# Input transposes evicted by plain copies, scaled rows made in SBUF, the decay polynomial traced later

## The chip, the core and the metric

The kernel runs on one core of a Trainium2 chip. The metric is the device time of one execution in microseconds (us). Engines are named as in the profile: PE (matrix engine), DVE (vector), ACT (scalar), POOL (GpSimd) and SP, which here only issues DMAs. They run side by side, each through its own instructions in a fixed order, and meet at semaphores.

## What is computed

Two layers of a hybrid trunk over 640 tokens (512 noisy latents and 128 prompt tokens) of width 1024. Cut to what matters here:

```python
def layer(x, cvec, ctx, norm_g, w_mod, b_mod, w_in, ...):
    mod = silu(cvec) @ w_mod + b_mod
    shift, scale, gate = split(mod, 3)
    h = rms_norm(x, norm_g) * (1 + scale) + shift
    rq, rk, rv, rz, q_lat, kv_lat, k_r, ... = split(h @ w_in)
    # three branches: retention, latent attention, Fourier mixing
    ...
    x = x + gate * (merged @ w_out)
```

The retention branch also needs `log_sigmoid(ret_decay_logit)`, 16 numbers.

## The kernel before

All activations are kept transposed: eight tiles of 128 channels by 640 tokens. Every matrix product is made of three passes over a high and a low part of both operands (`hh`, `hl` for the hidden rows, `wh`, `wl` for weights); ACT makes the high part with a cast (L78), DVE or POOL the low part with a subtraction (L74).

The change lies in the opening stage of layer 0. SP loads five token tiles `xn` (L1159, 512 KB each), then, in groups, the first two thirds of `w_mod` in sixteen chunks of 512 KB (`mraw`, L175) and the latents' input weights (`raw`, L92). Then:

- ACT squares each `xn` tile and sums it (L1162); POOL turns the sums into inverse norms `rin` (L1163, L1164).
- PE spreads `rin` over the partitions (`bcast`, L245, five transposes into a PSUM buffer `big`), and ACT copies that to `nR` in SBUF (L247).
- For each of the eight channel blocks d, PE transposes five 128x128 tiles into a `big` buffer (L1170). There are two `big` buffers. ACT copies the block to `xt` (L1172, kept for the residual), and DVE multiplies the same PSUM block by `nR` into `xr` (L1173).
- `mod_use` (L187, L196, L200, L204) multiplies the `w_mod` chunks. Two chunks make one of eight blocks of the shift and scale vectors `modT`: four matmuls for each chunk into the PSUM tile `fill`, a copy by ACT (L192), two small matmuls (L196) and one or two DVE additions.
- `scaled` (L1155) applies scale and shift to `xr`, and `split` makes `hh` and `hl`.
- The latents (`lat_mm`, L85, L86, L87) follow: 120 matmuls of 384 columns for the queries' part, and 120 of 288 columns for the keys' part, with `hh`/`hl` as stationary operand.

Apart from that, the 16 decay logits `lg` go through a chain of some 28 tiny DVE operations and two ACT exponentials (L147 to L169); the results `lgc`, `lg` and `dec` are first read in the retention stage, hundreds of us later.

The order of instructions on each engine is not the order of the code. A scheduler in the build (`schedule_with_timeline_sim=True`) places every instruction by its own estimate of times, by the order in which the code traces them where that leaves a choice. It runs over the whole program, so an edit at the start can also move rows much later. After the build the order is fixed; an engine never passes an instruction that waits.

Of the kernel before, what the change touches and what calls it, by code (L numbers as in the profile page):

```python
# [20 lines left out]
NT = 5
# [9 lines left out]
def build(nc, tc, A, O):  # L31
    ACT, DVE, POOL, PE = nc.scalar, nc.vector, nc.gpsimd, nc.tensor
    root = ExitStack()

    def pool(stack, name, bufs=1, **kw):
        return stack.enter_context(tc.tile_pool(name=name, bufs=bufs, reuse_waits="tile", **kw))

    cp = pool(root, "cp")
# [13 lines left out]
    def big():  # L52
        return psum["p"].tile([P, 1024], F32, name="big", tag="big", bufs=2)
# [67 lines left out]
    prep = pool(pre, "pre")  # L121
# [5 lines left out]
    lg = cp.tile([P, 16], F32, name="lg")  # L127
    nc.scalar.dma_start(lg, A["ret_decay_logit"].rearrange("l d h -> (l d h)").partition_broadcast(P))
    expo = cp.tile([P, 2], F32, name="expo")
# [11 lines left out]
    ACT.activation(cth, cT, AF.Tanh, scale=0.5)  # L141
    DVE.scalar_tensor_tensor(cth, cth, 1.0, cT, op0=ALU.add, op1=ALU.mult)
    DVE.tensor_scalar(cs[:, 0:2 * NK].rearrange("p (k c) -> p k c", c=2), cth.rearrange("p c k -> p k c"), 0.5, None, op0=ALU.mult)


    ab = cp.tile([P, 16], F32, name="ab")
    DVE.scalar_tensor_tensor(ab, lg, -1.0, lg, op0=ALU.mult, op1=ALU.max)  # L147
    ey = cp.tile([P, 16], F32, name="ey")
    ACT.activation(ey, ab, AF.Exp, scale=-1.0)
    DVE.tensor_scalar(ab, ey, 2.0, None, op0=ALU.add)  # L150
    DVE.reciprocal(ab, ab)
    DVE.tensor_tensor(ey, ey, ab, op=ALU.mult)
    DVE.tensor_tensor(ab, ey, ey, op=ALU.mult)
    pl = cp.tile([P, 16], F32, name="pl")
    DVE.memset(pl, 1.0 / 19.0)
    for n in (17, 15, 13, 11, 9, 7, 5, 3, 1):
        DVE.tensor_tensor(pl, pl, ab, op=ALU.mult)
        DVE.tensor_scalar(pl, pl, 1.0 / n, None, op0=ALU.add)
    DVE.scalar_tensor_tensor(pl, pl, -2.0, ey, op0=ALU.mult, op1=ALU.mult)
    DVE.scalar_tensor_tensor(lg, lg, 0.0, pl, op0=ALU.min, op1=ALU.add)  # L160
    lgv = lg.rearrange("p (l d h) -> p l d h", l=2, d=2)
    lgc = cp.tile([P, 2, 2, 2], F32, name="lgc")
    lgp = lg.rearrange("p (l d h e) -> p l d h e", l=2, d=2, e=2)
    for e in range(2):
        DVE.tensor_copy(lgc[64 * e:64 * e + 64], lgp[64 * e:64 * e + 64, :, :, :, e])
    dec = cp.tile([P, 2, 2, 4], F32, name="dec")
    for d in range(2):
        DVE.tensor_scalar(dec[:, :, d, :], lgv[:, :, d, :], expo[:, d:d + 1], None, op0=ALU.mult)
    ACT.activation(dec, dec, AF.Exp)  # L169

    modT = [cp.tile([P, 24, 2], F32, name=f"modT{l}") for l in range(DEPTH)]

# [68 lines left out]
    def bcast(tp, r, t0, t1):  # L241
        a, b = t0 * P, t1 * P
        pb = big()
        for t in range(t0, t1):
            ins = PE.transpose(pb[:, t * P:(t + 1) * P], r[:, t:t + 1].to_broadcast([P, P]), ident)  # L245
        R = tp.tile([P, TT], F32, name="nR", tag="nR", bufs=1)
        ACT.copy(R[:, a:b], pb[:, a:b])  # L247
        return R, ins
# [93 lines left out]
    def lat_w(l, i):  # L342
        return wload(rows(A["w_in"][l], 2 * i, 2, C_LAT, 384), 2, 384, DVE)
# [808 lines left out]
    def scaled(d):  # L1152
        v = xrs[d]
        for c, s_ in ((0, slice(0, T)), (1, slice(T, TT))):
            DVE.tensor_scalar(v[:, s_], v[:, s_], modT[0][:, 8 + d, c:c + 1], modT[0][:, d, c:c + 1], op0=ALU.mult, op1=ALU.add)  # L1155
        split(hh[d], hl[d], v, leng=POOL if d % 2 else DVE)
# [3 lines left out]
    rin = prep.tile([P, NT], F32, name="rin")  # L1160
# [1 line left out]
        ACT.activation(omt.rearrange("p w n -> p (w n)")[:, 0:D], xn[t], AF.Square, scale=D ** -0.5, accum_out=rin[:, t:t + 1])  # L1162
    POOL.tensor_scalar(rin, rin, EPS, None, op0=ALU.add)  # L1163
    POOL.tensor_tensor(rin, rin, mhalf[:, 0:NT], op=ALU.pow)  # L1164
    R, _ = bcast(prep, rin, 0, NT)
    xts, xrs = [], []
    for d in range(NK):
        ps = big()
        for t in range(NT):
            PE.transpose(ps[:, t * P:(t + 1) * P], xn[t][:, d * P:(d + 1) * P], ident)  # L1170
        xt, xr = (prep.tile([P, TT], F32, name=f"{n}{d}") for n in ("xt", "xr"))
        ACT.copy(xt, ps[:, :TT])  # L1172
        DVE.tensor_tensor(xr, ps[:, :TT], R, op=ALU.mult)  # L1173
        xts.append(xt)
        xrs.append(xr)
    for i in range(4):
        for b in (4 + i, i):
            for j in range(0, NK, 4):
                mod_use(0, b, j, mod_load(0, b, j, prep, 256, 256, 4, 10, nc.sync), 256, 4, po1[:, 4 * b:])
        first.append(lat_w(0, i))  # L1180
        for d in (2 * i, 2 * i + 1):
            scaled(d)
    xstore = [nc.sync.dma_start(xd[0][d], xts[d]) for d in range(NK)]
    pre.close()

    acc = None
    for l in range(DEPTH):
# [26 lines left out]
        with ExitStack() as s:  # L1214
# [57 lines left out]
            for n, (idx, src, tmp) in enumerate(((1, omt, None), (0, ort, om), (2, ort, om))):  # L1272
# [5 lines left out]
                for i in range(4):  # L1278
# [14 lines left out]
                    ps = tmp[0:2] if n else ms  # L1293
# [13 lines left out]
        with ExitStack() as s:  # L1307
            xp = pool(s, f"xo{l}")
            xts = []
# [6 lines left out]
            xts = orr + off  # L1316
# [20 lines left out]
            for t0, t1, order in passes:  # L1337
                a, b = t0 * P, t1 * P
                for d in order:
                    xo, xt = om[d % 4], xts[d]  # L1340
                    nc.sync.dma_start(xo[:, a:b], xd[l][d][:, a:b])
                    ps, ins = out_mm(d, a, b)
                    if l + 1 < DEPTH and t0 == 0 and d == order[0]:
                        with tc.issue_after(ins.ins):
                            R, _ = bcast(xp, rms(xp, xts, *passes[0])[0], 2, 5)
                        make_h(l + 1, xp, xts, R, 2, 5)
                    for c, i, j in ((0, a, min(b, T)), (1, T, b)):
                        if j > i:
                            DVE.scalar_tensor_tensor(xt[:, i:j], ps[:, i - a:j - a], modT[l][:, 16 + d, c:c + 1], xo[:, i:j],
                                                     op0=ALU.mult, op1=ALU.add)  # L1350
# [12 lines left out]
                if l + 1 < DEPTH:  # L1363
                    if t0 == 0:
# [13 lines left out]
                        with tc.issue_after(ins.ins):  # L1378
                            R, ins = bcast(xp, r, t0, t1)
# [80 lines left out]
```

## Time and profile before

| what | value |
|---|---|
| median of three runs | 1472.1 us (1469.72 to 1475.49) |
| the profiled execution's own time | 1475.04 us |
| its span, first to last instruction | 1473.3 us |
| PE busy | 1411.6 us (96%) |
| DVE, ACT, POOL busy | 1025.5, 756.2, 239.1 us |
| mean granted PE clock | 0.993 |

PE is the engine to follow: it is busy nearly the whole span. Idle time of another engine costs nothing unless PE waits at its end. In the profile, matmul records overlap, since they are pipelined: the pace is read from one start to the next, not from the duration.

### The profile page before, as it was taken

How to read it: one execution, taken by the hardware profiler on the slowest of the kernel's cores; microseconds unless marked ns; L12 is line 12 of the kernel's file. 1: busy time of each engine (PE TensorE's matmuls, PEld its weight loads, DVE VectorE, ACT ScalarE, POOL GpSimd, SP SyncE). 2: the span in 40 equal slices, each digit the busy share in tenths (PEclk: the TensorE clock that was granted, in tenths of full speed). 3: DMA queues.
4: the chain of work that ended last, by engine and by line, in shares of the span. 5: the costliest groups of instructions: out<-in, count | busy, mean ns of one | idle time of the engine just before them, and what ended most of it. 6: DMA issues, size and time to landing. Idle time of an engine off the chain costs nothing.

```text
span 1473.3 us, 25184 instructions
## 1 busy us (share of the span) xinstructions
PE 1411.6 (96%) x9793; PEld 1345.2 (91%) x9793; DVE 1025.5 (70%) x1896; ACT 756.2 (51%) x1607; POOL 239.1 (16%) x227
## 2 busy tenths in 40 slices
PE   6999999999999999999999999999999999999997
PEld 4989989988988989999999899899889899999997
DVE  5367776666887686698573777765759778779843
ACT  5546666544545453455354566664545445445542
POOL 1220000301102211122312100021110112112240
PEclk9999999999999999999999999999999999999999
DMA  9520003331325474233532100042222433323342
GB/s 317 179 76 1 15 16 98 102 84 33 94 90 176 130 221 129 57 85 92 166 101 84 33 15 16 15 138 77 73 73 65 146 108 104 94 80 86 90 125 87
DMA packets 175847, 138.91 MB, mean 94 GB/s; under 512 B 8304, under 2 KB 168688, under 8 KB 175728
## 3 DMA queue, kind: packets, MB, share of 16 engines
q1 hardware_dynamic: 157680, 120.16, 28.1%
q10 hardware_dynamic: 18048, 17.15, 3.7%
q8 instruction: 77, 1.26, 0.4%
q14 instruction: 42, 0.34, 0.1%
HBM read 125.98 MB, written 11.30 MB: 93 GB/s over the span
## 4 chain that ended last, share of the span: by engine, by line
PE 74%; DVE 12%; DMA 5%; ACT 4%; issue 4%; POOL 1%; SPq 0%; POOLq 0%; ACTq 0%; DVEq 0%
PE bank L1109 25%; PE sm L85 6%; PE sm L87 5%; PE sm L86 5%; PE big L269 4%; PE bank L1080 4%; PE big L513 4%; PE fill L319 3%; PE sm L319 3%; PE sm L534 2%; PE sm L526 2%; DVE wl L74 2%; PE fill L187 2%; DMA raw<-in_w_in 1%; PE big L411 1%
## 5 line engine op out<-in xcount | busy, mean ns | idle before, releaser
L74 DVE TENSOR_TENSOR wl<-raw,wh 128x1024 fp32r<-128x1024 f32 (+5 forms) x146 | 153.8, 1055 | 87.3 <-ACT wh L78 39.0
L78 ACT CAST wh<-raw 128x1024 fp32r<-128x1024 f32 (+5 forms) x126 | 104.7, 833 | 86.2 <-DMA raw<-in_w_in 27.9
L1109 PE MATMUL bank<-hh,wh 128*128 128x320 f32 x416 | 130.0, 315 | 5.5 <-ACT tg L1125 4.4
L85 PE MATMUL sm<-wh,hh 128*128 128x256 f32 (+2 forms) x456 | 134.2, 295 | 0.5 <-DVE vl L74 0.5
L86 PE MATMUL sm<-wl,hh 128*128 128x256 f32 (+2 forms) x456 | 133.8, 294 | 0.0
L87 PE MATMUL sm<-wh,hl 128*128 128x256 f32 (+2 forms) x456 | 132.6, 294 | 0.0
L1109 PE MATMUL bank<-hl,wh 128*128 128x320 f32 x416 | 128.6, 310 | 0.0
L1109 PE MATMUL bank<-hh,wl 128*128 128x320 f32 x416 | 127.1, 311 | 0.0
L74 POOL TENSOR_TENSOR wl<-raw,wh 128x1024 fp32r<-128x1024 f32 (+1 forms) x32 | 66.4, 2075 | 294.9 <-ACT wh L78 215.7
L74 POOL TENSOR_TENSOR wl<-st,wh 128x512 fp32r<-128x512 f32 x26 | 38.0, 1463 | 328.8 <-ACT wh L78 328.8
L85 PEld LDWEIGHTS sm<-wh,hh 128*128 128x128 f32 x456 | 87.8, 193 | 2.2 <-issue 0.8
L1109 PEld LDWEIGHTS bank<-hh,wh 128*128 128x128 f32 x416 | 78.3, 188 | 11.9 <-ACT tg L1125 5.2
L86 PEld LDWEIGHTS sm<-wl,hh 128*128 128x128 f32 x456 | 87.8, 193 | 0.1
L87 PEld LDWEIGHTS sm<-wh,hl 128*128 128x128 f32 x456 | 87.4, 192 | 0.4 <-issue 0.4
L1109 PEld LDWEIGHTS bank<-hl,wh 128*128 128x128 f32 x416 | 78.5, 189 | 0.0
L1109 PEld LDWEIGHTS bank<-hh,wl 128*128 128x128 f32 x416 | 78.0, 189 | 0.0
L74 DVE TENSOR_TENSOR ptl<-sm,pth 128x384 fp32r<-128x384 f32 x128 | 67.2, 549 | 13.9 <-ACT pth L78 12.9
L1109 PE MATMUL bank<-bq,wh 128*128 128x320 f32 x320 | 72.0, 311 | 0.0
L78 ACT CAST pth<-sm 128x384 fp32r<-128x384 f32 x128 | 57.2, 481 | 22.6 <-PE sm L526 21.8
L78 ACT CAST wh<-st 128x512 fp32r<-128x512 f32 x68 | 39.6, 618 | 55.1 <-PE bank L1109 53.7
L640 DVE TENSOR_REDUCE nm<-big 128x1 f32<-128x768 f32 x64 | 60.7, 948 | 1.7 <-PE big L513 1.6
L74 DVE TENSOR_TENSOR wl<-st,wh 128x512 fp32r<-128x512 f32 x42 | 40.8, 972 | 29.5 <-ACT wh L78 27.0
(578 smaller groups left out, 4540.3 us busy)
## 6 DMA issues: line engine op xcount, KB each, us to landing
raw<-in_w_in SPq DMA_DIRECT2D x96, 512.0 KB, 4.0
mraw<-in_w_mod ACTq DMA_DIRECT2D x32, 512.0 KB, 4.0
raw<-in_w_branch SPq DMA_DIRECT2D x24, 512.0 KB, 3.6
mraw<-in_w_mod SPq DMA_DIRECT2D x16, 512.0 KB, 9.2
raw<-in_w_out SPq DMA_DIRECT2D x16, 512.0 KB, 4.3
raw<-in_w_in SPq DMA_DIRECT2D x8, 384.0 KB, 6.1
om<-xd SPq DMA_DIRECT2D x16, 192.0 KB, 3.5
xd<-xt SPq DMA_DIRECT2D x8, 320.0 KB, 4.2
```

Source lines behind the costliest of these rows:

```text
L74: eng.tensor_tensor(lo, src, hi.bitcast(F32), op=ALU.subtract)
L78: ACT.copy(hi, src)
L85: PE.matmul(out, ah, bh, start=first, stop=False)
L86: PE.matmul(out, ah, bl, start=False, stop=False)
L87: return PE.matmul(out, al, bh, start=False, stop=last)
L187: PE.matmul(ps[c:c + 32, :n], cs[:, 2 * (j + i):2 * (j + i) + 32], rv[:, i, :], start=(j + i < 4), stop=(j + i >= 4), tile_position=(0, c))
L269: PE.matmul(ps[:, 512 * h:512 * h + 320], ws[a][:, k, :], xs[b][k][:, 320 * h:320 * h + 320], start=(first and k == 0 and i == 0), stop=(l ...
L319: PE.matmul(ps, w[a][:, k, :], (hh, hl)[b][k][:, hs], start=(k == 0 and i == 0), stop=(k == NK - 1 and i == 2))
L513: PE.matmul(S[:, 512 * h:512 * h + 384], qT[hd][a][:, t * P:(t + 1) * P], (kth, ktl)[b][hd % 3][:, 384 * h:384 * h + 384], start=(i == 0), ...
L640: DVE.tensor_reduce(nm, Sv, axis=AX.XY if len(Sv.shape) == 3 else AX.X, op=ALU.max, negate=True)
L1080: PE.matmul(A, ws[u][:, k, j * P:(j + 1) * P], xs[k][v][:, h, :], start=(k == 0 and i == 0), stop=(k == 3 and i == 2))
L1109: PE.matmul(ps, w[u], x[v], start=(first and k == 0 and j == 0), stop=(k == n - 1 and j == 2), skip_group_check=True)
```

## The change

Three edits, all traced in the opening stage:

1. The block loop no longer multiplies out of PSUM. Each transposed block is only copied to `xt`, by ACT for odd d and by DVE for even d.
2. `bcast` is traced after the eight blocks, and eight DVE multiplications then make `xr` out of `xt` in SBUF.
3. The decay logits' chain is traced after the loop over the `mod_use` blocks and the latents' weights, no longer before everything.

```diff
-    ab = cp.tile([P, 16], F32, name="ab")
-    DVE.scalar_tensor_tensor(ab, lg, -1.0, lg, op0=ALU.mult, op1=ALU.max)
...
-    ACT.activation(dec, dec, AF.Exp)
...
-    R, _ = bcast(prep, rin, 0, NT)
     xts, xrs = [], []
     for d in range(NK):
         ps = big()
         for t in range(NT):
             PE.transpose(ps[:, t * P:(t + 1) * P], xn[t][:, d * P:(d + 1) * P], ident)
         xt, xr = (prep.tile([P, TT], F32, name=f"{n}{d}") for n in ("xt", "xr"))
-        ACT.copy(xt, ps[:, :TT])
-        DVE.tensor_tensor(xr, ps[:, :TT], R, op=ALU.mult)
+        if d % 2:
+            ACT.copy(xt, ps[:, :TT])
+        else:
+            DVE.tensor_copy(xt, ps[:, :TT])
         xts.append(xt)
         xrs.append(xr)
+    R, _ = bcast(prep, rin, 0, NT)
+    for d in range(NK):
+        DVE.tensor_tensor(xrs[d], xts[d], R, op=ALU.mult)
     for i in range(4):
...
+    ab = cp.tile([P, 16], F32, name="ab")
+    DVE.scalar_tensor_tensor(ab, lg, -1.0, lg, op0=ALU.mult, op1=ALU.max)
...
+    ACT.activation(dec, dec, AF.Exp)
```

What the scheduler makes of it shows at three places. In the rows, `xn_87` to `xn_91` are the five token tiles, `fill<-mraw` is one chunk of `w_mod` (x4: its four matmuls), `sm<-sel,mraw` the small matmuls that close a block. Line numbers of the changed kernel differ: L1143 is L1170 of before, L161 is L187, L170 is L196, L219 is L245, L1153 is L1173, L1129 is L1155.

PE, the first matmuls of the program, before:

```order
L133 MATMUL sm<-ident,vecs 128x128
L187 MATMUL fill<-mraw,cs 32x256 x4
L245 MATMUL big<-ident,rin 128x128 x5
L1170 MATMUL big<-ident,xn_87 128x128
L1170 MATMUL big<-ident,xn_88 128x128
```

and after:

```order
L133 MATMUL sm<-ident,vecs 128x128
L1143 MATMUL big<-ident,xn_87 128x128 x2
L1143 MATMUL big<-ident,xn_88 128x128 x2
L1143 MATMUL big<-ident,xn_89 128x128 x2
L1143 MATMUL big<-ident,xn_90 128x128 x2
L1143 MATMUL big<-ident,xn_91 128x128 x2
```

The transposes of the first two blocks now stand ahead of the first chunk of `w_mod` and of `bcast`.

PE, where the latents' matmuls begin (`hh_149` and `hh_112` are the same tile, `hh0`), before:

```order
L196 MATMUL sm<-sel,mraw 128x2 x2
L187 MATMUL fill<-mraw,cs 32x256 x4
L85 MATMUL sm<-wh,hh_149 128x384
L86 MATMUL sm<-wl,hh_149 128x384
L85 MATMUL sm<-wh,hh_149 128x384
L86 MATMUL sm<-wl,hh_149 128x384
L1170 MATMUL big<-ident,xn_87 128x128
```

and after:

```order
L170 MATMUL sm<-sel,mraw 128x2 x2
L161 MATMUL fill<-mraw,cs 32x256 x8
L219 MATMUL big<-ident,rin 128x128 x5
L170 MATMUL sm<-sel,mraw 128x2 x2
L161 MATMUL fill<-mraw,cs 32x256 x8
L170 MATMUL sm<-sel,mraw 128x2 x2
L161 MATMUL fill<-mraw,cs 32x256 x16
L85 MATMUL sm<-wh,hh_112 128x384
```

Before, the first latent matmul stood behind the seventh chunk of `w_mod` and with three blocks of transposes still to come; after, it stands behind the twelfth chunk and behind all transposes.

DVE, the rows up to the first scaling of a hidden row, before:

```order
L1173 TENSOR_TENSOR xr_211<-big,nR 128x640
L200 TENSOR_TENSOR modT_147<-sm,vT 128x4
L204 SCALAR_TENSOR_TENSOR modT_147<-modT_147,vT 128x4
L74 TENSOR_TENSOR wl<-raw,wh 128x768
L1173 TENSOR_TENSOR xr_221<-big,nR 128x640
L200 TENSOR_TENSOR modT_147<-sm,vT 128x4
L1155 TENSOR_SCALAR xr_211<-xr_211,modT_147 128x512
```

and after:

```order
L1153 TENSOR_TENSOR xr_166<-xt_165,nR 128x640
L1153 TENSOR_TENSOR xr_175<-xt_174,nR 128x640
L1153 TENSOR_TENSOR xr_184<-xt_183,nR 128x640
L1153 TENSOR_TENSOR xr_193<-xt_192,nR 128x640
L1153 TENSOR_TENSOR xr_202<-xt_201,nR 128x640
L1153 TENSOR_TENSOR xr_211<-xt_210,nR 128x640
L1153 TENSOR_TENSOR xr_220<-xt_219,nR 128x640
L1153 TENSOR_TENSOR xr_229<-xt_228,nR 128x640
L1129 TENSOR_SCALAR xr_166<-xr_166,modT_110 128x512
```

The scaling of the first block stood behind two multiplications by `nR`; it now stands behind all eight.

The decay chain's 28 DVE rows have kept their place near the start of DVE's order, with one copy of a transposed block (`xt_165`) among the last of them; the exponential of `dec` on ACT stands one copy later than before. SP's order up to the latents' weights is the same in both. From the latents to the end of layer 0's attention PE's rows are the same in both; from the Fourier stage on, and in layer 1, rows of the branch products and of the later `mod_use` chunks differ in places by some rows to some dozen.

## Rows read from the trace of the kernel before

**Rows 1.** The page: the span of the profiled execution.

```profile
span 1473.3 us, 25184 instructions
```

**Rows 2.** Windows: stretch, length, busy us (instructions) of each engine, clock, DMA share, GB/s.

```profile
0.00:14.30 14.30, 0.45 (x1) 0.18 (x1) 5.95 (x35) 7.35 (x13) 0.93 (x8) 1.00 0.77 263
14.30:34.20 19.90, 19.45 (x165) 13.87 (x166) 13.77 (x26) 11.73 (x21) 3.19 (x4) 1.00 1.10 351
34.20:72.35 38.15, 38.15 (x282) 35.85 (x281) 14.13 (x28) 18.26 (x42) 12.20 (x23) 1.00 0.59 197
72.35:100.00 27.65, 27.05 (x170) 25.96 (x168) 17.46 (x39) 13.65 (x25) 5.92 (x6) 1.00 0.28 81
```

**Rows 3.** Timeline of PE: start us, us, engine, line, operation, tiles, count, idle before.

```profile
14.41 1.08 PE L187 MATMUL fill<-mraw,cs 128*32 128x256 f32 x8 [11.13 <-DVE dec L168]
16.84 1.27 PE L1170 MATMUL big<-ident,xn 128*128 128x128 f32 x5
18.64 0.77 PE L1170 MATMUL big<-ident,xn 128*128 128x128 f32 x5
25.67 0.44 PE L85 MATMUL sm<-wh,hh 128*128 128x384 f32 x1
39.09 0.33 PE L87 MATMUL big<-wh,hl 128*128 128x384 f32 x1
41.00 0.34 PE L86 MATMUL big<-wl,hh 128*128 128x384 f32 x1
72.35 1.25 PE L403 MATMUL sm<-ident,latq 128*128 128x128 f32 x9
```

**Rows 4.** Timeline of SP's queue: issue start, us, of three chunks of `w_mod`.

```profile
16.68 1.42 SPq L175 DMA_DIRECT2D mraw<-in_w_mod  x1
22.50 1.34 SPq L175 DMA_DIRECT2D mraw<-in_w_mod  x1
23.96 1.35 SPq L175 DMA_DIRECT2D mraw<-in_w_mod  x1
```

**Rows 5.** DMA issues of those chunks, the first alone, then two: KB, us to landing.

```profile
mraw<-in_w_mod SPq DMA_DIRECT2D x1, 512.0 KB, 9.2
mraw<-in_w_mod SPq DMA_DIRECT2D x2, 512.0 KB, 9.7
```

**Rows 6.** Lines on DVE and ACT, 14 to 60 us: busy us, mean ns, idle.

```profile
L1173 DVE TENSOR_TENSOR xr<-big,nR 128x640 f32<-128x640 f32 x8 | 6.5, 816 | 4.6 <-ACT xt L1172 4.6
L1155 DVE TENSOR_SCALAR xr<-xr,modT 128x512 f32<-128x512 f32 x8 | 4.3, 542 | 0.1
L1155 DVE TENSOR_SCALAR xr<-xr,modT 128x128 f32<-128x128 f32 x8 | 2.7, 340 | 0.0
L74 DVE TENSOR_TENSOR hl<-xr,hh 128x640 fp32r<-128x640 f32 x4 | 3.3, 817 | 0.1
L78 ACT CAST hh<-xr 128x640 fp32r<-128x640 f32 x8 | 5.6, 732 | 2.4 <-DVE xr L1155 2.4
L247 ACT COPY nR<-big 128x640 f32<-128x640 f32 x1 | 0.7, 693 | 2.6 <-PE big L245 2.6
```

**Rows 7.** Lines on PE, 15.6 to 75 us: busy us, mean ns, idle.

```profile
L187 PE MATMUL fill<-mraw,cs 128*32 128x256 f32 x120 | 9.0, 390 | 0.0
L1170 PE MATMUL big<-ident,xn 128*128 128x128 f32 x40 | 6.5, 298 | 0.0
L196 PE MATMUL sm<-sel,mraw 128*128 128x2 f32 x32 | 4.3, 237 | 0.1
```

**Rows 8.** Windows of PE: a sparse stretch of the attention, and what follows.

```profile
100.00:103.00 3.00, 1.36 (x6) 1.00 0.66 177
103.00:107.00 4.00, 3.83 (x11) 0.57 0.04 8
```

**Rows 9.** Windows of the stages whose order also differs, columns as in rows 2.

```profile
300.00:450.00 150.00, 142.11 (x978) 133.27 (x977) 114.13 (x246) 71.73 (x158) 15.67 (x20) 0.99 0.28 78
450.00:475.00 25.00, 21.62 (x159) 19.03 (x159) 18.14 (x31) 12.26 (x24) 6.06 (x4) 1.00 0.58 179
```

More of the change, by code (lines that the diff above doesn't have):

```diff
@@ L143, in build @@
     DVE.tensor_scalar(cs[:, 0:2 * NK].rearrange("p (k c) -> p k c", c=2), cth.rearrange("p c k -> p k c"), 0.5, None, op0=ALU.mult)
-    ab = cp.tile([P, 16], F32, name="ab")
-    DVE.scalar_tensor_tensor(ab, lg, -1.0, lg, op0=ALU.mult, op1=ALU.max)
[L148 to L168, printed above, removed]
-    ACT.activation(dec, dec, AF.Exp)
     modT = [cp.tile([P, 24, 2], F32, name=f"modT{l}") for l in range(DEPTH)]
@@ L1182, in build @@
             scaled(d)
+    ab = cp.tile([P, 16], F32, name="ab")
+    DVE.scalar_tensor_tensor(ab, lg, -1.0, lg, op0=ALU.mult, op1=ALU.max)
+    ey = cp.tile([P, 16], F32, name="ey")
+    ACT.activation(ey, ab, AF.Exp, scale=-1.0)
+    DVE.tensor_scalar(ab, ey, 2.0, None, op0=ALU.add)
+    DVE.reciprocal(ab, ab)
+    DVE.tensor_tensor(ey, ey, ab, op=ALU.mult)
+    DVE.tensor_tensor(ab, ey, ey, op=ALU.mult)
+    pl = cp.tile([P, 16], F32, name="pl")
+    DVE.memset(pl, 1.0 / 19.0)
+    for n in (17, 15, 13, 11, 9, 7, 5, 3, 1):
+        DVE.tensor_tensor(pl, pl, ab, op=ALU.mult)
+        DVE.tensor_scalar(pl, pl, 1.0 / n, None, op0=ALU.add)
+    DVE.scalar_tensor_tensor(pl, pl, -2.0, ey, op0=ALU.mult, op1=ALU.mult)
+    DVE.scalar_tensor_tensor(lg, lg, 0.0, pl, op0=ALU.min, op1=ALU.add)
+    lgv = lg.rearrange("p (l d h) -> p l d h", l=2, d=2)
+    lgc = cp.tile([P, 2, 2, 2], F32, name="lgc")
+    lgp = lg.rearrange("p (l d h e) -> p l d h e", l=2, d=2, e=2)
+    for e in range(2):
+        DVE.tensor_copy(lgc[64 * e:64 * e + 64], lgp[64 * e:64 * e + 64, :, :, :, e])
+    dec = cp.tile([P, 2, 2, 4], F32, name="dec")
+    for d in range(2):
+        DVE.tensor_scalar(dec[:, :, d, :], lgv[:, :, d, :], expo[:, d:d + 1], None, op0=ALU.mult)
+    ACT.activation(dec, dec, AF.Exp)
     xstore = [nc.sync.dma_start(xd[0][d], xts[d]) for d in range(NK)]
```

## The prediction

> **What bounds the kernel now.** I read the page first, then a table of windows over the opening stage, then PE's timeline in it, and last the DMA queue. The span is 1473.3 us [rows 1], the profiled execution took 1475.0 us, which is 2.9 us over the median of 1472.1, so what I add to the one I add to the other. The windows show two different limits in the first 72 us [rows 2]. Up to 14.3 us PE has done 0.45 us of work; it waits for its first chunk of `w_mod`. From 14.3 to 34.2 us the sixteen DMA engines are full (share 1.10, 351 GB/s), and PE is busy too, 19.45 of 19.9 us. From 34.2 to 72.35 us PE is busy without a gap, 38.15 of 38.15 us, and the DMA share has fallen to 0.59. The last latent matmul ends where the first transpose of `latq` starts, at 72.35 us [rows 3], and PE then goes on nearly without idle time, 27.05 of 27.65 us up to 100 us [rows 2]. So the time at which PE ends the latents is handed on to everything behind, nearly one to one. The whole change is judged by that one time.
>
> Two things in PE's timeline matter for it [rows 3]. The first latent matmul starts at 25.67 us: before, the latents are mixed with the transposes and with the chunks of `w_mod` that have already landed, so PE always has work while chunks are on their way. And the first work is slow: five transposes take 1.27 us at 16.84 us and 0.77 us at 18.64 us.
>
> **The change part by part.** *Transposes earlier.* The forty transposes now need only the token tiles and a free PSUM buffer. Ten of them start as the tiles land, up to 12.9 us, in time in which PE was idle. The other thirty start from some 14 us on. That takes work forward out of the stage from 14.3 us on. It is worth something only if PE then has something else to do earlier, and that is the question.
>
> *Where the first latent matmul stands.* In PE's new order it stands behind the twelfth chunk of `w_mod`, before it stood behind the seventh. PE cannot pass a waiting row, so no latent matmul starts before the twelfth chunk has landed. SP's order there is unchanged and the DMA engines are full, so I take the landings from the trace. The eighth chunk is issued at 16.68 us and lands 9.2 us later, at 25.9 us; the eleventh and twelfth are issued at 22.50 and 23.96 us and land 9.7 us later, at 32.2 and 33.7 us [rows 4, 5]. One chunk costs PE 9.0 us / 15 = 0.60 us [rows 7]. So the first latent matmul cannot start before 33.7 + 0.6 = 34.3 us, against 25.67.
>
> *What PE has to do meanwhile.* All transposes, `bcast`, eight chunks and four of the small closing steps stand ahead. From 14.2 us these are six blocks of transposes at some 0.7 us (4.2), eight chunks (4.8), `bcast` (0.7) and four closings of about 0.5 (4.3 us / 8 [rows 7]), 11.7 us in all and perhaps 2 more while PE is slow: PE is through with them about when the eighth chunk has been used and closed, at 27.2 us. From there to 34.3 us it has four chunks of 0.6 us, 2.4 us of work in 7 us.
>
> *The sum at 34.3 us.* What counts is the work that is left then. Before, 24 of the 240 latent matmuls were done by 34.2 us (4, 6, 2 and 12 rows of PE's order); after, none. They are of the 384-column kind, whose pace is (41.00 - 39.09) / 11 = 0.174 us [rows 3], so 24 are 4.2 us. Against that, before still had six chunks ahead and the new order has four: 2 x 0.60 = 1.2 us less. The closings left are four in both. Net: 4.2 - 1.2 = **+3.0 us** at PE's full rate.
>
> *PE's clock.* [...] I take **+1.7 us**, with nothing as the low end and twice that as the high end. [...]
>
> *`xr` from SBUF.* A 128x640 multiplication out of PSUM takes 816 ns, a subtraction of the same size wholly in SBUF 817 ns [rows 6], so the eight cost the same, 6.5 us. They now stand in one row behind `nR`. Their pace is about 0.74 us, since records overlap, so `hh0` is ready 8 x 0.74 (5.9), one scaling pair (0.54 + 0.34 = 0.88, some 0.75 by pace) and the cast (0.73) after `nR`, 7.4 us. `nR` comes when `bcast` and a 0.69 us copy are done. `bcast` stands behind six chunks, two closings and all transposes: 14.2 + 4.2 + 3.6 + 1.0 + 2 us for the slow start = 25.0 us, then 0.7 for itself and 0.7 for the copy: 26.4 us, so `hh0` at 33.8 us. This is half a us before 34.3 us: hidden by the wait for the twelfth chunk, but only just.
>
> *Four copies from ACT to DVE.* About 0.8 us each (as the 816 ns above); ACT and DVE both have room before 26 us (11.7 and 13.8 of 19.9 us [rows 2]). Nothing.
>
> *The decay chain.* Its DVE rows keep their place, in time in which DVE waits for `xn`, and its results are read in the retention stage. Nothing.
>
> *Later rows.* From the Fourier stage on the order differs by some rows. PE is idle 7.9 us between 300 and 450 us and 3.4 us between 450 and 475 us [rows 9]; a shift of rows can win or lose a part of this, and I take 0 with 2 us either way. What could swallow the delay is idle time of PE before that, 0.6 us up to 100 us [rows 2].
>
> Sum: 3.0 + 1.7 = 4.7 us, so 1475.0 + 4.7 = 1479.7 us for a profiled execution like the one shown, and 1472.1 + 4.7 = **1476.8 us** for the median. That is 0.32%. About 0.5%, 7.4 us, is what a measurement of this kernel can tell from no change, so the likeliest result is no change that can be told, on the slow side.
>
> **The rivals.** *DVE's row of eight becomes the bound (slower).* If `nR` comes later than 26.9 us, `hh0` and not the twelfth chunk starts the latents, and every further us is a us of the total. The mechanism is PE's slow start: at 1.27 in place of 0.77 us for a block and 1.08 us for a chunk [rows 3], thirty transposes and six chunks would take 7.6 + 6.5 us, not 4.2 + 3.6, if the clock stayed down up to `bcast`. Then `nR` comes at 14.2 + 14.1 + 1.0 + 1.4 = 30.7 us, `hh0` at 38.1 us, 3.8 us after the chunk. Price: 3.0 + 1.7 + 3.8 = 8.5 us, 1480.6 us. For it: only half a us of cover, and two PSUM buffers whose release now alternates between ACT and DVE, where a late one stalls the next block. Against it: before, PE was at full rate at 18.04 us or so after 3.6 us of work, and its work here is as dense.
>
> *The early transposes win (faster).* If chunks landed sooner than PE gets to them, the transposes' work, 6.5 us of records [rows 7], some 5.6 us by pace, would leave the full stretch: 1466.5 us. Against it: the landings, which hang on 351 GB/s of a full DMA system [rows 2], and nothing in the change moves a byte.
>
> *The clock holds.* Then only +3.0 us: 1475.1 us.
>
> *The change does nothing.* The delay is swallowed by idle time between 100 and 475 us, where PE waits on other engines: 1472 us. Those waits hang on work that is itself delayed, so I give it little.
>
> **How the numbers follow.** Forecast as summed, 0.45, with the later rows' 2 us either way: about a sixth of it ends beyond 7.4 us. Clock holds 0.17. DVE bound, in full or in part, 0.20, nearly all beyond 7.4 us. Nothing 0.12. Early transposes win 0.06, of which most is beyond 0.5%. Slower: 0.07 + 0.18 = 0.25. Faster: 0.05. Same: 0.70. The range has to leave out 2 in 10: from 1470.5 us (nothing, with the later rows winning) to 1483 us (DVE bound in full, with the later rows losing); outside lie the early transposes' win, a part of the case of nothing, and the worst of DVE's case.
>
> **What would show it.** In the changed kernel's profile: transposes at 7 to 13 us; PE busy about a third from 27 to 34 us, with rows of `w_mod` matmuls each waiting for a DMA; the first latent matmul (L85) at 34.3 us, with the twelfth chunk as the last thing waited for; a granted clock near one half for some 3 to 4 us around there; the first transpose of `latq` at 77 us in place of 72.35. If L85 starts at 34 us but waits for ACT's `hh`, DVE was the bound. If it starts well before 33 us, my landings or the reading of the order are wrong, and the prediction with them. If `latq` comes at 77 us and the total is unchanged, the delay was swallowed later.

## The result and the profile after

The changed kernel takes 1481.31 us in the median (1479.08 to 1485.22), the kernel before beside it 1471.56 us. The ratio is 1.0070, with a 95% interval of 1.0054 to 1.0086; by the medians it is 9.8 us or 0.66% slower. The time lies in the range that was given. It is twice the step that was forecast, though, and the forecast's likeliest case, no change that can be told, did not come.

The profiled execution of the changed kernel took 1484.34 us. The page gives its span (before: [rows 1]):

```profile
span 1482.5 us, 25171 instructions
```

The windows of the opening, columns as in [rows 2] (stretch, length, then busy us and count of PE, PEld, DVE, ACT and POOL, granted clock, DMA share, GB/s):

```profile
0.00:14.30 14.30, 3.99 (x12) 1.74 (x13) 5.68 (x31) 7.66 (x14) 0.95 (x8) 1.00 0.78 261
14.30:27.00 12.70, 11.56 (x111) 7.32 (x111) 6.93 (x18) 5.31 (x12) 1.23 (x2) 1.00 1.10 353
27.00:34.20 7.20, 5.09 (x37) 1.61 (x38) 7.20 (x14) 2.63 (x5) 0.96 (x1) 0.54 1.09 349
34.20:38.00 3.80, 3.80 (x16) 3.25 (x20) 3.80 (x8) 2.42 (x4) 1.62 (x2) 0.50 1.10 351
38.00:42.00 4.00, 4.00 (x22) 3.30 (x14) 0.48 (x1) 0.83 (x1) 1.88 (x1) 0.60 0.81 269
42.00:77.00 35.00, 35.00 (x245) 33.97 (x245) 11.17 (x24) 15.70 (x38) 11.13 (x22) 1.00 0.45 147
```

Before 14.3 us PE now does 4 us of work instead of 0.45. From 27 to 34.2 us it is busy 5.1 of 7.2 us, and at a clock of 0.54, so this is not even 3 us of work at the full rate. From 34.2 us on PE is busy without a gap, but up to 42 us at 0.50 and 0.60, against 1.00 behind that. (The clock column reads 1.00 in the first rows too, but PE still runs at half pace there: a chunk takes 1.08 us at 15.46 us and 0.64 us at 17.54 us. I do not use the column before 18 us.)

PE's timeline of the changed kernel (start us, us, engine, line, operation, tiles, count, idle before; L161 is the `w_mod` chunk, L170 the small matmuls that close a block, L85 and L86 the latents, L219 `bcast`, L377 the first transpose of `latq`; before: [rows 3]). Each matmul of a chunk and of a closing counts twice in the profile, so a chunk's four show as x8:

```profile
23.48 0.76 PE L219 MATMUL big<-ident,rin 128*128 128x128 f32 x5
...
25.91 0.64 PE L161 MATMUL fill<-mraw,cs 128*32 128x256 f32 x8 [0.69 <-DMA mraw<-in_w_mod]
27.04 0.61 PE L170 MATMUL sm<-sel,mraw 128*128 128x2 f32 x4 [0.49 <-ACT mraw L166]
28.54 1.08 PE L161 MATMUL fill<-mraw,cs 128*32 128x256 f32 x8 [0.90 <-DMA mraw<-in_w_mod]
29.96 1.08 PE L161 MATMUL fill<-mraw,cs 128*32 128x256 f32 x8 [0.34 <-DMA mraw<-in_w_mod]
31.57 1.08 PE L161 MATMUL fill<-mraw,cs 128*32 128x256 f32 x8 [0.53 <-ACT mraw L166]
32.96 1.08 PE L161 MATMUL fill<-mraw,cs 128*32 128x256 f32 x8 [0.31 <-DMA mraw<-in_w_mod]
33.97 0.69 PE L85 MATMUL sm<-wh,hh 128*128 128x384 f32 x1
...
36.27 0.52 PE L85 MATMUL big<-wh,hh 128*128 128x384 f32 x1
36.59 0.52 PE L86 MATMUL big<-wl,hh 128*128 128x384 f32 x1
...
41.32 0.34 PE L86 MATMUL sm<-wl,hh 128*128 128x384 f32 x1
41.49 0.34 PE L87 MATMUL sm<-wh,hl 128*128 128x384 f32 x1
...
78.48 1.25 PE L377 MATMUL sm<-ident,latq 128*128 128x128 f32 x9
```

The chunks come one by one, and PE waits before each; at 31.57 us it is ACT's copy of the block before (L166) that ends the wait, at the others the DMA. The first latent matmul starts at 33.97 us, right behind the twelfth chunk. Neighbouring latent matmuls stand 0.32 us apart at 36 us and 0.17 us apart at 41 us: the same instruction at a granted clock of 0.50 (36 to 37 us) and of 1.00 (41.2 to 42 us). `latq` follows at 78.48 us, against 72.35 before: **+6.1 us**. By this reading 6.1 of the 9.8 us are lost in the opening, and the other 3.6 us come later.

DVE's timeline of the changed kernel in that stretch, and ACT's casts that make the first two `hh` (columns as above; L1153 is `xr` from SBUF, L1129 the scaling):

```profile
25.00 5.97 DVE L1153 TENSOR_TENSOR xr<-xt,nR 128x640 f32<-128x640 f32 x8
30.89 1.51 DVE L1129 TENSOR_SCALAR xr<-xr,modT 128x512 f32<-128x512 f32 x4
33.99 2.74 DVE L1129 TENSOR_SCALAR xr<-xr,modT 128x512 f32<-128x512 f32 x4
...
31.73 1.44 ACT L78 CAST hh<-xr 128x640 fp32r<-128x640 f32 x2 [0.24 <-DVE xr L1129]
```

The eight multiplications run in one row, and the first scaling follows at 30.89 us. ACT's two casts are done at 33.17 us, the first of them, `hh0`, about 0.7 us earlier. What PE's first latent matmul reads at 33.97 us has by then been ready for more than 1 us, so DVE is not what the latents wait for.

### The profile page after: what moved, and what is told of

Same layout as the page of the kernel before. It is cut to its first block, busy times and chain, and to the rows that moved or that the text cites. A ratio compares the mean times of both kernels' runs of the same rounds, so it can differ in the third digit from the quotient of the medians.

```text
span 1482.5 us, 25171 instructions
## 1 busy us (share of the span) xinstructions
PE 1420.9 (96%) x9793; PEld 1349.2 (91%) x9793; DVE 1028.9 (69%) x1900; ACT 755.7 (51%) x1603; POOL 240.2 (16%) x227
## 4 chain that ended last, share of the span: by engine, by line
PE 75%; DVE 11%; DMA 5%; ACT 4%; issue 4%; POOL 1%; SPq 0%; POOLq 0%; ACTq 0%; DVEq 0%
PE bank L1083 26%; PE sm L85 6%; PE sm L87 6%; PE sm L86 6%; PE bank L1054 4%; PE big L487 4%; PE fill L293 3%; PE big L243 3%; PE sm L293 3%; PE sm L508 3%; PE sm L500 2%; PE fill L161 2%; DVE wl L74 2%; DMA s<-in_state_ret 1%; PE big L385 1%
## 5 line engine op out<-in xcount | busy, mean ns | idle before, releaser
L85 PE MATMUL sm<-wh,hh 128*128 128x256 f32 (+2 forms) x456 | 135.6, 298 | 1.0 <-DVE vl L74 0.9
L86 PE MATMUL sm<-wl,hh 128*128 128x256 f32 (+2 forms) x456 | 135.3, 297 | 0.0
L85 PEld LDWEIGHTS sm<-wh,hh 128*128 128x128 f32 x456 | 88.8, 195 | 2.9 <-DVE vl L74 1.4
L86 PEld LDWEIGHTS sm<-wl,hh 128*128 128x128 f32 x456 | 88.9, 195 | 0.1
```

Source lines behind the costliest of these rows:

```text
L85: PE.matmul(out, ah, bh, start=first, stop=False)
L86: PE.matmul(out, ah, bl, start=False, stop=False)
```

## The experiments

**Theory.** The changed kernel loses by the place of the first latent matmul in PE's fixed order (behind the twelfth chunk of `w_mod`, which lands at 33 us) and by the clock that the thin stretch before it brings down. **Rival:** the edits cost by themselves: copies on DVE, multiplications out of SBUF, the polynomial. A second question came with the totals: what are the 3.6 us behind `latq`?

The median of each kernel (5 to 12 runs) stands beside that of runs of the kernel before on the same chip; e9_before_rows and e10_lazy ran on a second chip. The ratio is not taken from the medians, so the two can differ by 1 us or so. "Rest" is the difference of the medians less the shift of `latq`. `latq` is read in one profiled execution of each kernel, and three kernels with the same order on every engine (changed, e2_nopoly, e10_lazy) have it 1.2 us apart, so a rest is good to some 2 us and no better.

| kernel | first latent behind chunk | first latent, us | `latq`, us (shift) | median less before | ratio (95%) | rest |
|---|---|---|---|---|---|---|
| before | 7 | 25.67 | 72.35 | | | |
| changed | 12 | 33.97 | 78.48 (+6.1) | +9.8 | 1.0070 (1.0054 to 1.0086) | +3.6 |
| e1_poly | 7 | 25.65 | 72.33 (0.0) | -0.3 | 1.0005 (0.9992 to 1.0018) | -0.3 |
| e2_nopoly | 12 | 34.79 | 78.67 (+6.3) | +9.4 | 1.0073 (1.0054 to 1.0091) | +3.1 |
| e3_gate | 12 | 33.72 | 74.15 (+1.8) | +6.2 | 1.0051 (1.0033 to 1.0068) | +4.4 |
| e4_warm | 12 | 34.93 | 77.09 (+4.7) | +2.6 | 1.0024 (1.0012 to 1.0035) | -2.1 |
| e5_copies | 8 | 28.29 | 73.08 (+0.7) | +1.7 | 1.0007 (0.9997 to 1.0017) | +1.0 |
| e6_held | 9 | 29.98 | 75.64 (+3.3) | +5.2 | 1.0039 (1.0024 to 1.0055) | +1.9 |
| e7_held_b1 | 7 | 25.96 | 72.89 (+0.5) | +1.5 | 1.0009 (0.9996 to 1.0021) | +0.9 |
| e8_held_b3 | 8 | 26.52 | 73.42 (+1.1) | +2.1 | 1.0020 (1.0008 to 1.0032) | +1.0 |
| e9_before_rows | 7 | 25.62 | 75.78 (+3.4) | +7.5 | 1.0049 (1.0037 to 1.0061) | +4.1 |
| e10_lazy | 12 | 34.12 | 77.50 (+5.2) | +8.5 | 1.0053 (1.0040 to 1.0066) | +3.4 |
| e11_bcast | 8 | 26.34 | 71.02 (-1.3) | -0.6 | 1.0003 (0.9989 to 1.0018) | +0.7 |

### One edit at a time: the polynomial

e1_poly is the kernel before with this alone:

```diff
-    ab = cp.tile([P, 16], F32, name="ab")
...
-    ACT.activation(dec, dec, AF.Exp)
...
         for d in (2 * i, 2 * i + 1):
             scaled(d)
+    ab = cp.tile([P, 16], F32, name="ab")
...
+    ACT.activation(dec, dec, AF.Exp)
```

> The kernel before with the third edit alone: the decay polynomial is traced behind the latents' inputs, nothing else is changed. PE's first latent matmul stands behind the seventh chunk of w_mod, as before. Theory (the place of the first latent matmul and the clock after the sparse stretch make the loss): the first transpose of latq at 72.4 us as before, ratio 1.000, within 2 us of the kernel before, by later rows alone. Rival (the polynomial's move costs, through the rows that it moves later): some +2 to +4 us of the 9.75, ratio 1.002 or more, and that from after 900 us.

e2_nopoly is the changed kernel with the polynomial back at its old place.

> The changed kernel with the polynomial back in its old place: edits 1 and 2 alone. PE's first latent matmul stands behind the twelfth chunk. Theory: opening as in the changed kernel, first latent matmul at 34.0 us and latq at 78.5 us, ratio 1.007 (1.004 to 1.009). Rival (the polynomial is a part of it): ratio about 1.004 with latq at 78.5 us, or latq well before 78.5 us.

Measured: 1.0005 and 1.0073, `latq` at 72.33 and 78.67 us. PE's order is in e1_poly that of before and in e2_nopoly that of the changed kernel. The polynomial is worth nothing that these runs can tell, and the loss belongs to edits 1 and 2.

### The place alone

e3_gate is the kernel before, with nothing but an order: the latents' matmuls of `hh0` are put behind the twelfth chunk.

```diff
+        if l == 0 and b == 2 and j == 4:
+            twelfth[1] = twelfth[0]
...
-                    lat_mm(acc[t], t, k, *w[k // 2], k % 2)
+                    if k == 0:
+                        with tc.issue_after(twelfth[1].ins):
+                            lat_mm(acc[t], t, k, *w[k // 2], k % 2)
```

> The kernel before with no edit to copies, multiplications or polynomial; only the first latent matmuls (those of hh0) are held behind the last matmul of the twelfth chunk in PE's order. Theory: the place alone makes the loss. First latent matmul at 34.0 to 34.3 us; the work left is then as in the changed kernel, +3.0 us, so latq at 75.4 us if the clock holds (here transposes are spread up to the tenth chunk, so PE is less idle before 34 us) and at up to 78.5 us if it falls as in the changed kernel; ratio 1.002 to 1.006. Rival (the row of eight multiplications on DVE, or the copies, delay the latents): without them nothing is lost, latq within 1 us of 72.4, ratio 1.000.

PE's timeline and windows of e3_gate (L1177 transposes, L188 a chunk, L199 a closing, L85 the first latent matmul, L410 the first transpose of `latq`):

```profile
28.78 0.77 PE L1177 MATMUL big<-ident,xn 128*128 128x128 f32 x5 [0.85 <-DVE xr L1180]
31.38 0.61 PE L199 MATMUL sm<-sel,mraw 128*128 128x2 f32 x4 [0.49 <-ACT mraw L195]
33.15 0.64 PE L188 MATMUL fill<-mraw,cs 128*32 128x256 f32 x8 [0.59 <-DMA mraw<-in_w_mod]
33.72 0.44 PE L85 MATMUL sm<-wh,hh 128*128 128x384 f32 x1
74.15 1.26 PE L410 MATMUL sm<-ident,latq 128*128 128x128 f32 x9
```

```profile
27.00:34.20 7.20, 5.07 (x53) 3.29 (x54) 6.52 (x14) 4.54 (x9) 1.78 (x2) 1.00 1.09 351
34.20:38.00 3.80, 3.80 (x28) 3.79 (x30) 0.96 (x1) 0.91 (x2) 0.78 (x1) 1.00 1.10 351
```

The first latent matmul again comes at 33.72 us, behind the same chunk, although nothing was changed on copies or multiplications. The clock is 1.00 throughout. PE has more to do in the thin stretch here (53 rows from 27 to 34.2 us where the changed kernel has 37), since some transposes stand later in this order. The place without the clock costs 1.8 us, less than the 3.0 that I had put down and far less than the changed kernel's 6.1. So the place is one part, and the clock, which stayed up here, can be the other. The whole is nevertheless 6.2 us slower: the rest, +4.4 us, is the largest of all, with an order of the later rows that is neither that of before nor that of the changed kernel.

### Work added to keep the clock up

e4_warm is the changed kernel with 16 matmuls more, of chunks 8 to 11 into an unused half of a PSUM buffer:

```diff
+    spare = []
...
+        if l == 0 and (b, j) in ((1, 4), (6, 0), (6, 4), (2, 0)):
+            for i in range(kk):
+                c = 32 * i
+                PE.matmul(spare[1][c:c + 32, 512:768], cs[:, 2 * (j + i):2 * (j + i) + 32], rv[:, i, :], start=True, stop=True,
+                          tile_position=(0, c))
...
+    spare += [big(), big()]
```

> The changed kernel with added work: the matmuls of chunks 8 to 11 of w_mod are done a second time into an unused half of a PSUM buffer, 16 matmuls more, 2.4 us at full rate, in the time in which PE waits for the next chunk; the first latent matmul stays behind the twelfth chunk. Theory (the sparse stretch from 27 to 34 us lets the clock fall, and its return at 41 us costs 3.1 us): granted clock near 1.00 from 27 to 41 us, first latent matmul at 34.0 to 34.6 us, latq at 75.4 us, so the whole 3 us faster than the changed kernel, ratio to the kernel before about 1.0045, although there is more work. Rival (the half pace from 34 to 41 us has another cause than PE's idle time): the clock stays near 0.5 there, latq at 78.5 us or later by up to 1.2 us, ratio 1.007 or more.

PE's timeline and windows of e4_warm (L162 a chunk, L167 the added matmuls):

```profile
30.16 0.61 PE L167 MATMUL big<-mraw,cs 128*32 128x256 f32 x8
32.42 0.64 PE L167 MATMUL big<-mraw,cs 128*32 128x256 f32 x8 [1.65 <-DMA mraw<-in_w_mod]
33.92 1.08 PE L162 MATMUL fill<-mraw,cs 128*32 128x256 f32 x8 [0.42 <-DMA mraw<-in_w_mod]
34.93 0.69 PE L85 MATMUL sm<-wh,hh 128*128 128x384 f32 x1
```

```profile
27.00:34.20 7.20, 4.06 (x60) 1.98 (x60) 7.20 (x13) 2.59 (x5) 0.02 (x1) 0.97 1.09 351
34.20:38.00 3.80, 3.80 (x24) 3.06 (x20) 3.50 (x8) 1.93 (x4) 2.23 (x1) 0.61 1.10 351
38.00:42.00 4.00, 4.00 (x30) 3.59 (x27) 3.22 (x4) 0.54 (x1) 1.84 (x1) 1.00 0.85 261
```

The clock stays at 0.97 up to 34.2 us and is back by 38 us. In between it falls, after PE has waited 1.65 us for the eleventh chunk. The added matmuls read the chunk that they repeat, so they stand beside that chunk's own and none was left for this wait. So `latq` came at 77.09 us, not at the 75.4 us expected. Still, with more work it came 1.4 us sooner than in the changed kernel, although its latents began 1.0 us later (34.93 us). The low stretch was shorter: 3.8 x 0.39 = 1.5 us lost, against 3.8 x 0.50 + 4.0 x 0.40 = 3.5 us, an estimate from the windows. That the whole is 7.1 us faster than the changed kernel (+2.6 against +9.8) has another part, which lies behind `latq` (rest -2.1 against +3.6); its later rows, too, have an order of their own.

### Do the copies and the multiplications cost?

e5_copies is the kernel before with edit 1 alone; the multiplication stays in the loop, and `bcast` ahead of it:

```diff
-        ACT.copy(xt, ps[:, :TT])
-        DVE.tensor_tensor(xr, ps[:, :TT], R, op=ALU.mult)
+        if d % 2:
+            ACT.copy(xt, ps[:, :TT])
+        else:
+            DVE.tensor_copy(xt, ps[:, :TT])
+        DVE.tensor_tensor(xr, xt, R, op=ALU.mult)
```

> The kernel before with the copies alone: the blocks are copied to xt by ACT and DVE in turn, and xr is made from xt in SBUF, but each multiplication stays in the block loop and bcast stays ahead of it. In PE's order the transposes are all done after the tenth chunk of w_mod, and the first latent matmul stands behind that. Theory (the place of the first latent matmul decides): the tenth chunk lands near 30.7 us, so the latents begin some 5 us later than before, but with all transposes done; latq at 72.5 to 75 us. Rival (SBUF multiplications and copies on DVE cost by themselves): latq at 76 us or later, with PE waiting for xr or hh before the latents and not for a DMA.

The text has the place wrong: the first latent matmul stands behind the eighth chunk there, not the tenth. It started at 28.29 us, `latq` came at 73.08 us (+0.7), and the ratio is 1.0007. The rival asked for 76 us or later. Copies and multiplications out of SBUF cost next to nothing here.

e11_bcast is the changed kernel with a single line moved; all three edits stay:

```diff
-    R, _ = bcast(prep, rin, 0, NT)
...
+        if d == 1:
+            R, _ = bcast(prep, rin, 0, NT)
```

> The changed kernel with one line moved: bcast is traced behind the second block of transposes, not behind the eighth; copies, the row of eight multiplications out of SBUF traced behind the loop, and the polynomial's new place all stay. PE's first latent matmul then stands behind the eighth chunk of w_mod with all transposes ahead of it, and PE's order from the latents' end on is that of the kernel before, row for row. Theory (the changed kernel loses by the place of the first latent matmul, the clock behind it and the later rows' order, not by the copies and multiplications): first latent matmul near 26.5 us, clock 1.00, latq at 71 to 73.5 us, ratio 0.999 to 1.002. Rival (the copies and SBUF multiplications, or the polynomial's place, are what costs): latq at 76 us or later, ratio over 1.004.

PE's timeline, the windows and DVE's group for `xr` in e11_bcast (the group: partitions x elements, count | busy us, mean ns of one | idle before):

```profile
25.77 0.64 PE L161 MATMUL fill<-mraw,cs 128*32 128x256 f32 x8 [0.20 <-DMA mraw<-in_w_mod]
26.34 0.44 PE L85 MATMUL sm<-wh,hh 128*128 128x384 f32 x1
71.02 1.25 PE L377 MATMUL sm<-ident,latq 128*128 128x128 f32 x9
```

```profile
14.30:27.00 12.70, 12.31 (x115) 8.23 (x116) 10.21 (x25) 6.33 (x13) 1.18 (x1) 1.00 1.10 352
27.00:34.20 7.20, 7.11 (x51) 5.98 (x50) 6.97 (x12) 2.69 (x5) 3.79 (x2) 1.00 1.10 350
```

```profile
L1154 DVE TENSOR_TENSOR xr<-xt,nR 128x640 f32<-128x640 f32 x8 | 6.4, 820 | 2.4 <-ACT nR L221 2.4
```

This decides between the two. With `bcast` behind the second block of transposes, `nR` is there early, the latents begin at 26.34 us, PE is busy 7.11 of 7.2 us at a clock of 1.00 where the changed kernel was busy 5.09 at 0.54, and `latq` comes 1.3 us sooner than in the kernel before. The whole is 1.0003: the 9.8 us are gone with one line. (The line also brings the later rows back to the order of before, so this run does not tell the opening's part from the other.)

### Other ways to bring the latents forward

e6_held keeps all edits and `bcast` where the change put it, but holds each pair of multiplications behind the scaling of the pair ahead:

```diff
+        return ins
...
-    for d in range(NK):
-        DVE.tensor_tensor(xrs[d], xts[d], R, op=ALU.mult)
...
+            if d < 2:
+                DVE.tensor_tensor(xrs[d], xts[d], R, op=ALU.mult)
+            else:
+                with tc.issue_after(held.ins):
+                    DVE.tensor_tensor(xrs[d], xts[d], R, op=ALU.mult)
+            done = scaled(d)
+        held = done
```

> The changed kernel with all three edits, but each pair of xr multiplications after the first is kept behind the scaling of the pair ahead of it in DVE's order. The first latent matmul then stands behind the ninth chunk of w_mod, not the twelfth; PE's order from the latents' end on is that of the changed kernel, row for row. Theory (place and clock): the ninth chunk lands near 28.5 us, latents begin at 29 to 30 us, clock 1.00 or a short fall, latq at 72.5 to 75 us, 3.5 to 6 us better than the changed kernel. Rival 1 (the copies and SBUF multiplications cost by themselves): latq at 77 us or later. On the later rows: if the changed order of later rows costs some 3.5 us, as the totals less the openings of three kernels so far suggest, the whole is 3.5 us more than latq's shift, as it is in the changed kernel; if it costs nothing, the whole is latq's shift to within 1.5 us.

PE's timeline and a window of e6_held:

```profile
29.41 0.64 PE L161 MATMUL fill<-mraw,cs 128*32 128x256 f32 x8 [1.75 <-DMA mraw<-in_w_mod]
29.98 0.69 PE L85 MATMUL sm<-wh,hh 128*128 128x384 f32 x1
27.00:34.20 7.20, 4.93 (x28) 3.33 (x28) 7.20 (x13) 2.60 (x6) 3.71 (x1) 0.76 1.09 351
```

The first latent matmul moved from the twelfth chunk to the ninth and from 33.97 to 29.98 us, and `latq` came 2.8 us sooner, at 75.64 us, a little past the end of what I expected. PE waited 1.75 us for the ninth chunk, and the clock was low behind that (0.76 in the window). The rest is +1.9 us, between the 3.5 us that I expected of the later rows and the 1.5 us at most that I expected if they cost nothing.

e7_held_b1 and e8_held_b3 are e6_held with `bcast` traced behind the second and the fourth block.

> As the kernel with the multiplications held, and bcast traced behind the second block in place of the eighth. The first latent matmul stands behind the seventh chunk, as before, and the transposes are done before it. Theory: first latent matmul near 25.7 us, clock 1.00 throughout, latq at 70 to 72.4 us, since ten to fifteen transposes (1.4 to 2.1 us) are done before 14.3 us in idle time and none stands behind the latents' start; ratio 0.998 to 1.000. Rival (the copies cost by themselves): latq behind 73 us.

> As the one before, with bcast traced behind the fourth block. The first latent matmul stands behind the eighth chunk; from the latents' end on PE's order is that of the kernel before, row for row. Theory: first latent matmul near 26 to 27 us, clock 1.00, latq at 70 to 72.4 us, and since the later rows are those of before, the whole differs from the kernel before by latq's shift alone: 0 to 2 us faster, ratio 0.9985 to 1.000. Rival (the copies cost by themselves, or later rows are not what separates the totals): latq behind 73 us, or a whole that is over 2 us away from latq's shift.

Both expectations were too good by a us or so: `latq` at 72.89 and 73.42 us. The latents began in time (25.96 and 26.52 us, clock 1.00), but holding the multiplications back made a wait of its own. PE's timeline of e7_held_b1:

```profile
47.80 0.61 PE L87 MATMUL sm<-wh,hl 128*128 128x384 f32 x2 [1.16 <-DVE hl L74]
```

e8_held_b3 has the same wait, 1.21 us at 48.37 us. By its letter the 73.42 us of e8_held_b3 meets the rival's condition (behind 73 us), but e11_bcast, with the same copies and multiplications and without the hold, has no such wait and `latq` at 71.02 us.

e10_lazy traces the multiplications in pairs, just ahead of the scaling, without any hold:

```diff
-    for d in range(NK):
-        DVE.tensor_tensor(xrs[d], xts[d], R, op=ALU.mult)
...
         for d in (2 * i, 2 * i + 1):
+            DVE.tensor_tensor(xrs[d], xts[d], R, op=ALU.mult)
             scaled(d)
```

> The changed kernel with the eight xr multiplications traced in pairs, each just ahead of the scaling that reads it, and nothing to hold them there. The scheduler places them all in one row behind nR again, and every engine's order is that of the changed kernel. So all theories expect the changed kernel's time: ratio 1.006 to 1.008, latq at 78.5 us; a second set of runs of the same orders, to set the size of the part behind latq (theory of the later rows' order: 3 to 4 us over latq's shift; rival, chance of the runs: 0 to 2 us).

The order of every engine came out as in the changed kernel, the multiplications again eight in a row. The ratio is 1.0053, a little below the range that I gave, and `latq` came at 77.50 us; here the clock was back a little sooner (0.50 from 34.2 to 38 us, 0.90 from 38 to 42 us).

### What lies behind `latq`

From the Fourier stage on, PE's order in e2_nopoly, e6_held, e9_before_rows and e10_lazy is that of the changed kernel, row for row; in e1_poly, e8_held_b3 and e11_bcast it is that of the kernel before. The other four (e3_gate, e4_warm, e5_copies, e7_held_b1) each have an order of their own there. (Ahead of that stage one matmul of the attention, near 115 us, stands twelve rows later in e6, e8, e9 and e11 than in before, where the expectations of e6, e8 and e11 took all rows from the latents' end as equal.) e9_before_rows was made for the question: it is the kernel before, with the latents' matmuls traced inside the loop over the groups.

```diff
-            for k in range(NK):
-                for t in range(NT):
-                    lat_mm(acc[t], t, k, *w[k // 2], k % 2)
...
         for d in (2 * i, 2 * i + 1):
             scaled(d)
+            for t in range(NT):
+                lat_mm(acc0[t], t, d, *first[i], d % 2)
```

> The kernel before with its copies, multiplications and polynomial untouched; only the latents' matmuls are traced inside the loop over the groups. That leaves PE's opening as before up to the place after the thirteenth chunk of w_mod (first latent matmul behind the seventh chunk), and gives all later rows of PE, from the Fourier stage on, in the order of the changed kernel, row for row. So it has the opening of the one and the later rows of the other. Theory (the later rows' order makes the part of the loss that latq's shift does not hold, some 3.5 us of the 9.75): latq at 72.4 us, whole 2 to 4 us over the kernel before, ratio 1.0015 to 1.003. Rival (later rows' order costs nothing; what is over 6.1 us came with the delayed start itself, or by chance of the runs): latq at 72.4 us and ratio 0.999 to 1.001.

Its opening was not that of before after all: `latq` came at 75.78 us, as PE waits several times between 43 and 55 us, 2.2 us in all (0.90 us for `hl` at 49.81 us is the longest). The whole is 1.0049, 7.5 us, so the rest is +4.1 us, just past what the theory of the later rows asks for (2 to 4) and not the 0 of the rival.

Taken together: with the later rows of the changed kernel the rest is +3.6, +3.1, +1.9, +4.1 and +3.4 us, with those of before -0.3, +1.0 and +0.7 us. The two groups do not overlap, and they differ by 2.7 us in the mean (2.0 us if the ratios are used in place of the medians). The rest does not follow the delay of the opening: e4_warm is 4.7 us late at `latq` and has -2.1 us, e9_before_rows is 3.4 us late and has +4.1. So the medians suggest that the order of the later rows, which the scheduler changed, costs 2 to 3 us. It is not shown, since each rest carries the 2 us or so of its interval, and four more orders have rests from -2.1 to +4.4 us.

The traces bear it out in part only. The spans less `latq` are 1404.0, 1398.7, 1398.0, 1401.2 and 1400.5 us with the changed kernel's later rows (changed, e2, e6, e9, e10), and 1400.9, 1396.8, 1399.8 and 1398.9 us with those of before (before, e1, e8, e11): 1.4 us apart in the mean, and the groups overlap. Two executions with the same order differ by more than that (e1_poly's span is 1469.1 us, before's 1473.3 [rows 1], with `latq` at the same time). By PE's rows, the first long stretch in which the two orders differ (390 to 563 us in before) is 1.7 us shorter in the mean with the changed order, and the last (1110 to 1219 us) 2 to 3 us longer, by where its end is put. So what the new order wins in layer 0 it loses again in layer 1, and by the traces the net is some 1 us. The clock behind `latq` does not make the difference: it reads 0.50 for some 17 us in the profiled execution of before (in stretches of 3.4 us, as from 103.5 to 106.9 us) and for as long in that of the changed kernel, up to the last 10 us. What makes up the rest of the 3.6 us stays open.

## Why the prediction was right, and where it was not

*Transposes earlier are worth nothing by themselves*: right. PE did 4.0 us of work before 14.3 us, and the end of the latents moved the other way. In e11_bcast, where the latents begin in time, `latq` came 1.3 us sooner than before.

*The first latent matmul cannot start before 34.3 us, since it stands behind the twelfth chunk*: right, 33.97 us, with the DMA of that chunk the last thing waited for. PE was through with the rest at 27 us, as worked out.

*Net work left, +3.0 us*: right in the changed kernel. Its shift of 6.1 us less the 3.5 us of the clock is 2.6 us. In e2_nopoly the clock was 0.50 and 0.68 in the same two windows, which is 3.2 us, and leaves 3.1; in e10_lazy it is 2.3 and 2.9. In e3_gate, where a closing more was done by then, the same place cost 1.8 us.

*The clock, +1.7 us*: right in kind, mis-sized. No run with this opening shows 1.7 us: by the windows it cost 3.5, 3.2 and 2.3 us in the three kernels that have it; my upper end was 3.4. The 1.7 us were an estimate, 4 x 0.43, from the stretch at 103 us [rows 8], where the clock came back within 4 us. Here PE was dense from 32.96 us on, and the clock came back near 41 us. It had fallen (0.54 from 27 to 34.2 us) in a stretch with waits of 0.31 to 0.90 us. In e4_warm, with more work in the same stretch, the clock cost 1.5 us in place of 3.5.

*`xr` from SBUF at the same price*: right, 820 ns out of SBUF in e11_bcast against 816 ns out of PSUM [rows 6].

*DVE hidden, but only by half a us*: right in sign, and the cover was over 1 us. The rival in which the row of eight becomes the bound did not come. It needs PE slow up to `bcast`, and PE was at full pace from 17.5 us on (a chunk in 0.64 us at 17.54 us, 1.08 us at 15.46 us): `bcast` stood at 23.48 us and the row began at 25.00 us, where I had 26.4.

*Copies and polynomial, nothing*: right (1.0007 and 1.0005 alone).

*Later rows, 0 with 2 us either way*: this is the term that failed most. In the changed kernel +3.6 us lie behind `latq` (+3.1 and +3.4 in the two kernels with the same orders); that the later order makes 2 to 3 us of it is suggested by the runs and not shown. With the clock's 1.8 us more than forecast, this makes the other half of the 9.8 us, and puts the result beyond 0.5%.

So in the opening the mechanism was the one forecast, and the whole came as 2.6 + 3.5 + 3.6 us where the sum had 3.0 + 1.7 + 0. That the time still lies in the range is partly luck. With the upper ends of the clock (3.4) and of the later rows (2) the forecast reaches 1480.5 us, less than the 1481.31 us measured; what the range has above that was put there for DVE's row as the bound, and that did not happen. The 8.5 us of that rival are close to the 9.8 us by their size alone.

What remains argued and not shown is why the scheduler put the latents behind the twelfth chunk. That eight multiplications become ready at the same moment and are placed in one row, so that by its estimate `hh0` comes late, fits e6_held (held apart: ninth chunk) and e11_bcast (`nR` earlier: eighth chunk), but its estimates were not looked at.

## What to carry to other kernels

When a change moves work forward on an engine with a fixed order, look for the first big piece of work behind it and ask which DMA it now stands behind. The price is the work that is still undone when that DMA lands, and what the clock takes after the thin stretch (2.6 and 3.5 us here), neither the length of the work moved nor the delay of the start (8.3 us here, for a shift of 6.1). A value that many instructions wait for, as `nR` here, is best made as soon as its first reader can use it (e11_bcast); a scheduler that sees all readers ready at once may, it seems, run them all before the one that matters. And differences of 0.2% between versions of a kernel whose scheduler reorders later rows are not to be put down to the edit before neighbours with the same later order have been run.

## What the runs showed of the hardware

The clock came down in the changed kernel at 27.5 us, after waits of PE of only 0.69 and 0.49 us, with chunks used between them. It was back at about 41.2 us, after some 8 us in which PE had worked without a gap (windows of PE; columns as above):

```profile
27.00:27.50 0.50, 0.46 (x4) 1.00 1.01 334
27.50:28.00 0.50, 0.15 (x2) 0.53 1.04 346
40.00:41.00 1.00, 1.00 (x5) 0.50 0.90 310
41.00:41.50 0.50, 0.50 (x4) 0.81 0.44 152
```

In e8_held_b3 one wait of 1.06 us in otherwise dense work left the clock at 1.00 from 27 to 34.2 us; in e6_held, with one of 1.75 us, it was 0.76 in that window.

Some rows of DVE and POOL took longer where they ran side by side. DVE's and POOL's own rows from the changed kernel's timeline:

```profile
33.26 0.82 DVE L74 TENSOR_TENSOR hl<-xr,hh 128x640 fp32r<-128x640 f32 x1
33.24 2.24 POOL L74 TENSOR_TENSOR hl<-xr,hh 128x640 fp32r<-128x640 f32 x1 [17.63 <-ACT hh L78]
33.99 1.77 DVE L1129 TENSOR_SCALAR xr<-xr,modT 128x512 f32<-128x512 f32 x1
45.52 1.56 POOL L74 TENSOR_TENSOR hl<-xr,hh 128x640 fp32r<-128x640 f32 x1 [5.64 <-ACT hh L78]
```

A scaling of 128x512 took 1.77 us on DVE where it began during a subtraction of POOL's, and 0.54 to 0.55 us at the other seven places of the opening. POOL's subtraction took 2.24 us where it began together with one of DVE's (33.24 us), and 1.56 us where DVE was just ending its own (45.52 us); DVE's subtraction at 33.26 us took its usual 0.82 us. What made the rows longer is not shown: no run was made on it. PE waited for none of this in the changed kernel.
